# Splitting the first dense weights during the last experts, and the residual's scale and shift on VectorE

## The chip, the cores and the metric

The kernel runs on one core of a Trainium2 chip. The metric is the device time of one execution in microseconds (us), median of several runs. TensorE (PE) multiplies matrices into PSUM banks, VectorE (DVE), ScalarE (ACT) and GpSimd (POOL) do elementwise work, SyncE (SP) issues the weight transfers. Each engine works through its own queue in the order in which the program was written, and waits on semaphores of the others.

## The reference

A decoder trunk of two layers on 256 rows of width 1024, float32. Layer 0 is a retention layer, layer 1 a sparse-attention layer that reads keys and values projected from the rows after layer 0. Each layer ends with a mixture of 16 experts, two per row. Residual and norm stand behind each part:

```python
for l in range(DEPTH):                       # DEPTH = 2
    mix = retention(h, ...) if l == 0 else nsa_attention(h, ..., nsa_shared_kv(h, ...))
    h = layer_norm(ALPHA * h + mix, ln_mix_g[l], ln_mix_b[l])
    h = layer_norm(ALPHA * h + moe(h, ...), ln_ffn_g[l], ln_ffn_b[l])
```

What the change touches lies between the experts of layer 0 and the attention of layer 1: `layer_norm(..., ln_ffn_g[0], ln_ffn_b[0])`, the projections `h @ w_kv` and `h @ w_in`, and the residual `ALPHA * h` of layer 1.

## The kernel before

**Weights.** All weight matrices come as a list of chunks of 128 x 2048 float32 (1 MB): 32 dense chunks of the retention, 96 of the experts of layer 0 (six each), 18 dense chunks of the attention layer, 96 of the experts of layer 1. The class `Weights` brings them in through a ring of seven places, with more places lent for a time. `pump` (L75) issues the next transfer on SP as soon as a place is free. `self.next` counts half chunks (128 x 1024).

**Two kinds of chunk.** Expert chunks, and four dense ones, are multiplied as they are ("plain"). The other dense halves are first split into a high and a low part of the type fp32r, so that three fast matmuls replace one slow one: a copy on ACT (L114) and a subtraction on DVE (L115). The two parts go to one of four places of the pool `stage` (`self.slots`). `ahead` (L102) splits as many coming halves as there are free places, but none from `self.limit` on; `take` and `get` (L130, L139) call it each time PE's program asks for the next half and so gives back the last one's place. A split is thus written into the queues of ACT and DVE at the point where an older half is given up.

**Experts.** `experts` (L709) writes expert after expert. In round e, PE gets the matmuls of gate and up of expert e+1, with a few fillers (the transposes of the hidden rows of e, `turn`, and the scatter of expert e-1's result into the four sums `y`), then `down(e)`. The hidden rows of e+1 take one instruction on ACT (L790) and one on DVE (L791); the result of `down` is split by ACT (L217) and DVE (L218) before its scatter. While a layer's experts run, `self.limit` is 0, set in `mix_norm` (L597); behind the last expert it is lifted (L956). In layer 0 the function then calls `ahead(2, nc.gpsimd)` (L960): two halves are split with GpSimd in VectorE's role.

**Between the layers.** `next_rows` (L992) follows: 20 warming matmuls (L247), the statistics of the four sums and the reciprocal root on DVE (`block_stats`, L301 to L274), the normalised rows `res` (L1004 on ACT, L1005 on DVE), their transposes on PE (L1012), and per pair of transposes a high part on ACT (L1015) and a low part on DVE (L1017, L1021). It loads the norm's two rows `gb` through the POOL queue and returns the function that makes `res` the residual: `res * gb[0] + gb[1]` for both blocks of 128 rows.

**Attention layer, first part.** `nsa` (L1044) then runs five projections (`proj`, L322: 48 matmuls of 512 columns, four halves of weights each). Here they are called projection 1 to 5: 1 to 3 give keys and values, 4 and 5 the queries. `shift()` stands at L1231, ahead of projection 1. After projection 1 come `pairs` (ropes on DVE, L1068 to L1074, a copy on ACT, L1111), the gate weights and the router's sums; projection 2 is written behind these. Behind projection 4 the queries of block 0 get their rope on DVE; those of block 1 are copied by ACT to `qc` (L1255) and get theirs on GpSimd. `qc` takes the place (tag `q1`) that `gb` had. The residual itself is read only after the attention (L1457).

The order in each queue is the order of the program text (`manual_schedule`); nothing reorders it.

Of the kernel before, what the change touches and what calls it, by code (L numbers as in the profile page):

```python
# [23 lines left out]
NE = 16  # L24
# [129 lines left out]
class Trunk:  # L154
# [46 lines left out]
    def alloc(self, name, side="right"):  # L201

        self.extra.append(self.tc.alloc_tile_pool(name=name, bufs=1, side=side, reuse_waits="tile"))
        return self.extra[-1]

    def first_place(self, l, side):

# [501 lines left out]
    def experts(self, pool, keep, oh0, rest, hh, hl, y, l):  # L709
# [92 lines left out]
        def down(e, hT):  # L802

            b = [self.bank(), self.bank()]
            for k in range(4):
                both(hT[:, k, :], self.W.get(2)[0], b, k == 0, k == 3)
            if not out:
                out.append(self.first.tile([P, 2048], F32R, tag="raw", name=f"out{l}"))
            d = []
            for i in range(2):  # L810
                t = out[0][:, i * 512:i * 512 + 512]
                hi, lo = t[64 * i:64 * i + 64], t[64 - 64 * i:128 - 64 * i]
                self.hilo(hi, lo, b[i][64 * i:64 * i + 64, :])
                d.append(t)
            return d
# [111 lines left out]
        for e in range(NE):  # L927
            g = e // 4 + 1
            if e % 4 == 1 and g < 4:
                oh[g] = self.one_hot(keep, g, l)  # L930
                picks = gather(g)
            hT = pool.tile([P, 4, 64], F32, tag="hT", name=f"hT{l}_{e}", bufs=1)
            fill = [lambda: turn(hT)] + (scatter(e - 1, d, False) if e else [])
            if e % 4 == 0 and e:
                fill.append(lambda: turn_hot(e // 4))
            if e + 1 < NE:
                fill += more[:1] + picks[:2] + todo[:2]
                more, picks, todo = more[1:], picks[2:], todo[2:]
                b = gate_up(e + 1, fill)
                if e % 4 == 2 and g < 4:  # L940
                    weigh(g)
                hidden(e + 1, b)
            else:
                for f in fill:
                    f()
            if e == 13:
                overflow()
            d = down(e, hT)
            if e == 0:
                turn_hot(0)  # L950
            if l == 1 and e > 9 and self.gb is None and self.W.slots:
                todo += norm_rows()
        for f in todo:
            f()
        self.ready(AF.Sqrt)
        self.W.limit = 2 * len(self.W.srcs)  # L956
        for f in scatter(NE - 1, d, True):
            f()
        if l == 0:
            self.W.ahead(2, nc.gpsimd)  # L960

    def ffn(self, y, rows, keep, acc, l):

# [28 lines left out]
    def next_rows(self, pool, y, res, hTh, hTl):  # L992

        nc = self.nc
        self.gb = self.extra[0].tile([P, 2048], F32, tag="q1", name="gb1").rearrange("p (a n) -> p a n", a=2)
        nc.gpsimd.dma_start(self.gb, self.t["ln_rows"][1:2].to_broadcast([P, 2, 1024]))
        self.warm(self.bits, WARM[1])
        mv, ends = self.block_stats(pool, y, "lf0")
        rs = [f() for f in ends]
        mr = pool.tile([P, 1], F32, name="lf0_mr")  # L1000
        nc.vector.scalar_tensor_tensor(mr, mv[0][:, 0:1], -1.0, rs[0], op0=ALU.mult, op1=ALU.mult)
        for nh in range(2):
            c = slice(nh * 512, nh * 512 + 512)
            nc.scalar.activation(res[:, 0, c], y[0][nh], AF.Identity, bias=mr, scale=rs[0])  # L1004
            nc.vector.tensor_scalar(res[:, 1, c], y[1][nh], mv[1][:, 0:1], rs[1], op0=ALU.subtract, op1=ALU.mult)  # L1005
        o = W_LN + 16
        for j in range(0, 8, 2):
            b = self.bank().rearrange("p (a b) -> p a b", a=2)
            t = pool.tile([P, 2, 256], F32, tag="nt", name=f"nt{j}", bufs=2)
            for jj in range(2):  # L1010
                for tb in range(2):
                    nc.tensor.transpose(b[:, jj, tb * P:tb * P + P], res[:, tb, (j + jj) * P:(j + jj + 1) * P], self.ident)  # L1012
            gc = [[self.wsm[:, i + j + jj:i + 1 + j + jj] for i in (o, o + 8)] for jj in range(2)]
            for jj, (g, c) in enumerate(gc):
                nc.scalar.activation(hTh[:, j + jj], b[:, jj], AF.Identity, bias=c, scale=g)  # L1015
            for jj, (g, c) in enumerate(gc):
                nc.vector.tensor_scalar(t[:, jj], b[:, jj], g, c, op0=ALU.mult, op1=ALU.add)  # L1017
                if j == 0 or jj:
                    k = slice(jj if j == 0 else 0, jj + 1)
                    ks = slice(j + k.start, j + k.stop)  # L1020
                    nc.vector.tensor_sub(hTl[:, ks], t[:, k], hTh[:, ks].bitcast(F32))  # L1021
            if j == 4:
                self.W.ahead(1)
        return lambda: [self.scale_shift(nc.gpsimd, res[:, tb, :], res[:, tb, :], slice(0, 1024)) for tb in range(2)]

    def last_rows(self, pool, y):
        nc = self.nc
# [16 lines left out]
    def nsa(self, pool, norm, nq, keep):  # L1044
# [128 lines left out]
        def gate_logits():  # L1173
            b = self.bank()
            for k in range(8):
                for i, (w, x) in enumerate(((wgh, hTh), (wgh, hTl), (wgl, hTh))):
                    nc.tensor.matmul(b[0:48, 0:256], w[:, k, :], x[:, k, :], start=(k == 0 and i == 0), stop=(k == 7 and i == 2))
            ge = pr.tile([48, 256], F32, name="ge")
            nc.scalar.activation(ge, b[0:48, 0:256], AF.Exp, scale=-1.0)
            return ge  # L1180

        def set_gates(ge):
            b = self.bank()
            for tb in range(2):
                nc.tensor.transpose(b[:, tb * 48:tb * 48 + 48], ge[:, tb * P:tb * P + P], self.ident[0:48, 0:48])
            gv = flat(gates)
            nc.vector.tensor_scalar_add(gv, b[:, 0:96], 1.0)
            nc.vector.reciprocal(gv, gv)
# [3 lines left out]
        def turn_hidden(ck, cv):  # L1192
            b = self.bank()
            for a, c in enumerate((ck, cv)):
                for m in range(2):
                    nc.tensor.transpose(b[:, a * 128 + m * 64:a * 128 + m * 64 + 64], c[:, m * P:m * P + P], self.ident[0:64, 0:64])
            hk[0] = pr.tile([P, 2, 64], F32, name="hk")
            nc.vector.tensor_copy(hk[0], b[:, 0:128].rearrange("p (m r) -> p m r", m=2))
            hv[0] = pr.tile([P, 2, 4, 4, 32], F32, name="hv")
            nc.gpsimd.memset(hv[0], 0.0)  # L1200
            bv = b[:, 128:256].rearrange("p (m r) -> p m r", m=2)[:, :, 0:60].rearrange("p m (g n) -> p m g n", g=4)
            for m in range(2):
                nc.vector.tensor_copy(hv[0][:, m, :, :, 0:NCMP], bv[:, m].unsqueeze(2).to_broadcast([P, 4, 4, NCMP]))
# [24 lines left out]
        with self.phase("nkv") as pr:  # L1228
            wv = pr.tile([P, V_N], F32, name="wv")
            nc.gpsimd.dma_start(wv, self.t["w_nsa"])  # L1230
            shift()  # L1231
            KC = big.tile([P, 2048], F32, tag="q0", name="KC").rearrange("p (a g t) -> p a g t", a=2, g=4)
            b = self.proj(hTh, hTl, early=True)
            wgh, wgl = [pr.tile([P, 8, 48], F32R, name=f"wg{c}") for c in "hl"]
            kv2 = pairs(b)
            self.hilo(wgh, wgl, wv[:, V_GT:V_GT + 384].rearrange("p (k n) -> p k n", k=8))
            sums = self.router(pr, 1)
            b = self.proj(hTh, hTl)
            turn_pairs(kv2)
            t = [keys(0, tb, b[tb]) for tb in range(2)]  # L1240
            sums()
            blk = [blocks(0)]
            b = self.proj(hTh, hTl)
            for f in t:
                f()
            blk.append(blocks(1))
            t = [keys(1, tb, b[tb]) for tb in range(2)]
            ck = hidden(0, blk[0])
            cv = hidden(1, blk[1])
            ge = gate_logits()  # L1250
            QT = []
            b = self.proj(hTh, hTl, fill=[t[0], t[1], none, lambda: turn_hidden(ck, cv), lambda: set_gates(ge), none, compressed])
            t = [queries(0, 0, b[0])]
            c = big.tile([P, 2048], F32, tag="q1", name="qc")
            nc.scalar.copy(c[:, 0:512], b[1])  # L1255
            t.append(queries(0, 1, c[:, 0:512], nc.gpsimd, c[:, 512:1536]))
            t[0][0]()
            t = [t[0][1], *t[1]]
# [310 lines left out]
```

## Time and profile before

| | |
|---|---|
| median of 3 runs | 902.41 us (899.76, 902.41, 905.68) |
| profiled execution, its own time | 901.26 us |
| its span, first to last instruction | 899.4 us |
| mean granted TensorE clock | 0.977 of 2.4 GHz |
| busy in the span: PE / DVE / ACT / POOL | 849.5 / 407.7 / 339.8 / 67.4 us |

The page gives each engine's busy time, the span in 40 slices of 22.5 us, the chain of work that ended last, and the costliest groups of instructions. Two thin spots of PE stand out among the slices: the first slices of the run, and the two around 427 to 472 us. A closer look needs the timeline (instructions in order of time, with the idle time ahead of each and what ended it), short windows with the granted clock, and the instructions of one line.

### The profile page before, as it was taken

To read this page: it belongs to the slowest core of one execution; us is meant where nothing else is said; L and a number is where in the kernel's file an instruction comes from. 1 tells how busy PE (TensorE), PEld (TensorE's weight loads), DVE (VectorE), ACT (ScalarE), POOL (GpSimd) and SP (SyncE) were. 2 spreads that over 40 slices of the span, in tenths; PEclk is the share of its full clock that TensorE was granted. 3 is DMA by queue.
4 is the path that set the end of the run, shared out by engine and by line. 5 is a ranking of instruction groups with operands and counts; after the bars stand their busy time and mean duration, and the time that the engine had idled before them with its cause. 6 is when DMAs were issued, how large, how long until landed. Compare 5 with 4: busy or idle time off the path is not lost. (4 is left out here: it accounts for less than half of the span.)

```text
span 899.4 us, 12118 instructions
## 1 busy us (share of the span) xinstructions
PE 849.5 (94%) x4738; PEld 537.3 (60%) x4738; DVE 407.7 (45%) x811; ACT 339.8 (38%) x657; POOL 67.4 (7%) x76
## 2 busy tenths in 40 slices
PE   7999999998999999999779999899999999999993
PEld 5998989986545354453237777665844535445431
DVE  4667766864322222221169866885442222222215
ACT  4434344434232322322153555785433232232312
POOL 1000000001100000000036003430020000000001
PEclk8999999998999999999999899999999999999997
DMA  9956353588599999999723375303779999999901
GB/s 341 426 229 234 137 193 139 188 321 354 204 389 415 427 422 427 423 426 423 306 85 132 144 294 212 126 22 148 308 287 387 421 426 426 426 426 426 388 3 47
DMA packets 37282, 259.83 MB, mean 289 GB/s; under 512 B 4216, under 2 KB 4400, under 8 KB 6368
## 3 DMA queue, kind: packets, MB, share of 16 engines
q1 hardware_dynamic: 36432, 255.87, 70.3%
q0 software_dynamic: 640, 2.97, 1.0%
q8 instruction: 42, 0.69, 0.3%
q14 instruction: 24, 0.20, 0.1%
q10 hardware_dynamic: 144, 0.11, 0.1%
HBM read 257.88 MB, written 1.05 MB: 288 GB/s over the span
## 5 line engine op out<-in xcount | busy, mean ns | idle before, releaser
L771 PE MATMUL bank<-raw,xT 128*64 128x512 f32 x1024 | 233.9, 596 | 0.8 <-ACT xT L730 0.8
L771 PEld LDWEIGHTS bank<-raw,xT 128*64 128x64 f32 x1024 | 76.7, 137 | 125.9 <-issue 119.0
L115 DVE TENSOR_TENSOR st<-raw,st 128x1024 fp32r<-128x1024 f32 x90 | 114.9, 1304 | 51.1 <-ACT st L114 49.9
L114 ACT CAST st<-raw 128x1024 fp32r<-128x1024 f32 x92 | 94.6, 1048 | 78.0 <-PE bank L334 26.3
L771 PE MATMUL bank<-raw,hT 128*64 128x512 f32 x512 | 116.9, 594 | 7.2 <-PEq L875 3.3
L318 PE MATMUL bank<-xh,st 128*128 128x256 f32 x512 | 93.5, 284 | 3.0 <-ACT st L114 2.6
L218 DVE TENSOR_TENSOR out<-bank,out 64x512 fp32r<-64x512 f32 x64 | 44.1, 688 | 102.5 <-ACT out L217 101.5
L771 PEld LDWEIGHTS bank<-raw,hT 128*64 128x64 f32 x512 | 39.9, 137 | 74.1 <-issue 71.6
L318 PEld LDWEIGHTS bank<-xh,st 128*128 128x128 f32 x512 | 80.4, 192 | 3.6 <-ACT st L114 2.8
L217 ACT CAST out<-bank 64x512 fp32r<-64x512 f32 x64 | 37.1, 580 | 108.7 <-PE bank L771 107.9
L318 PE MATMUL bank<-xl,st 128*128 128x256 f32 x256 | 72.3, 282 | 0.0
L791 DVE SCALAR_TENSOR_TENSOR sh<-bank,wsl,sh 64x512 f32<-64x512 f32 x32 | 23.7, 741 | 105.3 <-ACT sh L790 105.1
L790 ACT ACTIVATE sh<-bank 64x512 f32<-64x512 f32 x32 | 19.0, 594 | 94.8 <-PE bank L771 94.8
L334 PE MATMUL bank<-st,hTh 128*128 128x512 f32 x128 | 45.8, 429 | 4.1 <-ACT st L114 2.2
L318 PEld LDWEIGHTS bank<-xl,st 128*128 128x128 f32 x256 | 49.4, 193 | 0.1
L351 PE MATMUL acc<-st,gh 128*128 128x512 f32 x128 | 43.2, 410 | 1.7 <-DVE st L115 1.1
L800 ACT COPY hT<-bank 128x256 f32<-128x256 f32 x32 | 12.0, 374 | 86.9 <-PE bank L799 86.8
L820 PE MATMUL y_moe<-out 128*128 128x512 f32 x128 | 38.6, 419 | 4.4 <-DVE out L218 4.4
L334 PE MATMUL bank<-st,xh 128*128 128x512 f32 x128 | 40.6, 393 | 0.0
L835 DVE SCALAR_TENSOR_TENSOR al<-bank,wsm,al 128x256 f32<-128x256 f32 x16 | 7.7, 484 | 72.1 <-ACT al L834 72.1
L728 DVE TENSOR_SCALAR xT<-bank,wsm 128x128 f32<-128x128 f32 x64 | 21.9, 405 | 34.1 <-PE bank L722 26.2
L334 PEld LDWEIGHTS bank<-st,hTh 128*128 128x128 f32 x128 | 25.7, 204 | 11.6 <-ACT st L114 2.6
(329 smaller groups left out, 1224.1 us busy)
## 6 DMA issues: line engine op xcount, KB each, us to landing
raw<-in_w_moe_dram SPq DMA_DIRECT2D x190, 1024.0 KB, 10.6
raw<-in_w_dense_dram SPq DMA_DIRECT2D x49, 1024.0 KB, 6.5
raw<-in_w_moe_dram SPq DMA_DIRECT2D x4, 512.0 KB, 15.8
xT<-in_x_T_dram SPq DMA_DIRECT2D x4, 256.0 KB, 4.6
raw<-in_w_dense_dram SPq DMA_DIRECT2D x2, 512.0 KB, 9.4
rt<-in_c_ret_dram POOLq DMA_DIRECT2D x1, 1024.0 KB, 11.1
gb<-in_ln_rows_dram POOLq DMA_DIRECT2D x1, 1024.0 KB, 6.4
out_dram<-lf_n SPq DMA_DIRECT2D x4, 256.0 KB, 2.0
```

Source lines behind the costliest of these rows:

```text
L114: self.nc.scalar.copy(hi, r)
L115: (eng or self.nc.vector).tensor_sub(lo, r, hi.bitcast(F32))
L217: self.nc.scalar.copy(hi, src)
L218: self.nc.vector.tensor_sub(lo, src, hi.bitcast(F32))
L318: self.nc.tensor.matmul(b[:, m, :], w[:, kk, c], x[:, k, :], start=(k == 0 and i == 0 and m == 0), stop=(k == 7 and i == 2 and m == 1))
L334: self.nc.tensor.matmul(b[tb], x[:, k, c], w[:, kk, :], start=(k == 0 and i == 0), stop=(k == 7 and i == 2))
L351: self.nc.tensor.matmul(y[tb][nh], x[a][:, c], w[b][:, 0, n], start=False, stop=last and i == 2)
L728: nc.vector.tensor_scalar(t, v, c, d, op0=ALU.mult, op1=ALU.add)
L771: nc.tensor.matmul(b[i][c, :], x, w[:, i, :], start=first, stop=last)
L790: nc.scalar.activation(rows[0:64], b[64:128], AF.Silu)
L791: nc.vector.scalar_tensor_tensor(rows[0:64], b[0:64], w, rows[0:64], op0=ALU.mult, op1=ALU.mult)
L820: return [lambda tb=tb, nh=nh: nc.tensor.matmul(y[tb][nh], o[:, tb, :], d[nh], start=(e == 0), stop=last) for nh in range(2) for tb in ran ...
```

## The change

Four edits:

1. New method `split_ahead(n)`: it sets the limit to n halves behind the experts of layer 0 and calls `ahead()`.
2. In layer 0, round 14 calls `split_ahead(2)` and round 15 `split_ahead(4)`, each just ahead of `down(e)`: dense halves 0 and 1, then 2 and 3, split by ACT and DVE.
3. The two splits with GpSimd behind the last expert go; the limit is lifted behind the last scatter.
4. The residual's scale and shift become two functions on VectorE, one per block of 128 rows. The first is written behind `gate_logits` and ahead of projection 4, the second as the last filler of projection 4. `shift()` ahead of projection 1, on GpSimd, goes.

```diff
+    def split_ahead(self, n):
+        self.W.limit = 2 * self.moe_end(0) + n
+        self.W.ahead()
...
             if e == 13:
                 overflow()
+            if l == 0 and e >= NE - 2:
+                self.split_ahead(2 * (e - NE + 3))
             d = down(e, hT)
...
         self.ready(AF.Sqrt)
-        self.W.limit = 2 * len(self.W.srcs)
         for f in scatter(NE - 1, d, True):
             f()
-        if l == 0:
-            self.W.ahead(2, nc.gpsimd)
+        self.W.limit = 2 * len(self.W.srcs)
...
-        return lambda: [self.scale_shift(nc.gpsimd, res[:, tb, :], res[:, tb, :], slice(0, 1024)) for tb in range(2)]
+        return [lambda tb=tb: self.scale_shift(nc.vector, res[:, tb, :], res[:, tb, :], slice(0, 1024)) for tb in range(2)]
...
             nc.gpsimd.dma_start(wv, self.t["w_nsa"])
-            shift()
             KC = big.tile([P, 2048], F32, tag="q0", name="KC").rearrange("p (a g t) -> p a g t", a=2, g=4)
...
             ge = gate_logits()
+            shift[0]()
             QT = []
-            b = self.proj(hTh, hTl, fill=[t[0], t[1], none, lambda: turn_hidden(ck, cv), lambda: set_gates(ge), none, compressed])
+            b = self.proj(hTh, hTl, fill=[t[0], t[1], none, lambda: turn_hidden(ck, cv), lambda: set_gates(ge), none, compressed, shift[1]])
```

## Rows read from the trace of the kernel before

**Rows 1.** Windows: us, busy PE, PEld, DVE, ACT, POOL; PEclk, DMA share, GB/s

```profile
468.00:470.00 2.00, 2.00 (x13) 1.77 (x11) 0.80 (x2) 1.92 (x6) 0.36 (x1) 0.61 1.00 418
474.00:476.00 2.00, 2.00 (x8) 1.57 (x7) 2.00 (x4) 0.08 (x1) 0.00 (x0) 0.69 0.00 0
...
494.00:496.00 2.00, 0.73 (x2) 0.30 (x2) 2.00 (x7) 2.00 (x3) 0.00 (x0) 0.93 0.02 4
502.00:504.00 2.00, 2.00 (x16) 1.99 (x15) 1.78 (x3) 0.96 (x2) 0.00 (x0) 0.86 0.64 270
```

**Rows 2.** Timeline behind the last expert: start, us, engine, line, operation [idle before]

```profile
459.49 1.89 DVE L301 BATCH_NORM_STATS2 lf_st<-y_moe 128x6 f32<-128x512 f32 x3
461.21 4.65 POOL L115 TENSOR_TENSOR st<-raw,st 128x1024 fp32r<-128x1024 f32 x2 [231.03 <-ACT st L114]
463.61 2.26 DVE L274 SCALAR_TENSOR_TENSOR lf_y<-lf_q,lf_y 128x1 f32<-128x1 f32 x1
466.31 0.15 DVE L1001 SCALAR_TENSOR_TENSOR lf_mr<-lf_mv,lf_y 128x1 f32<-128x1 f32 x1
467.42 2.75 PE L1012 MATMUL bank<-cst,res 128*128 128x128 f32 x16 [3.90 <-ACT res L1004]
470.77 1.19 PE L334 MATMUL bank<-st,hTh 128*128 128x512 f32 x2 [0.60 <-DVE nt L1017]
```

**Rows 3.** Chain that ended last: start, us, what (the kernel's final norm)

```profile
886.42 1.91 DVE lf_st L301 x3
...
890.74 0.15 DVE lf_mr L1033
```

**Rows 4.** Line L115 from 440 to 560 us: min/median/max ns, first and last start

```profile
L115 DVE TENSOR_TENSOR st<-raw,st x18: 1215/1227/3572, 474.3 to 546.8; 128x1024 fp32r<-128x1024 f32 x18
```

**Rows 5.** Timeline of projections 1 and 2, from 481 to 497 us

```profile
481.67 6.77 DVE L115 TENSOR_TENSOR st<-raw,st 128x1024 fp32r<-128x1024 f32 x2
...
484.08 0.39 PE L334 MATMUL bank<-st,hTh 128*128 128x512 f32 x1
484.31 0.40 PE L334 MATMUL bank<-st,hTl 128*128 128x512 f32 x1
487.44 3.26 POOL L990 TENSOR_TENSOR res<-res,gb 128x1024 f32<-128x1024 f32 x1
488.36 0.41 DVE L1068 TENSOR_TENSOR nr<-bank,rp 128x256 f32<-128x256 f32 x1
493.75 3.89 ACT L114 CAST st<-raw 128x1024 fp32r<-128x1024 f32 x4
494.85 0.50 PE L334 MATMUL bank<-st,hTh 128*128 128x512 f32 x1 [2.20 <-ACT st L114]
496.68 1.22 PE L334 MATMUL bank<-st,hTh 128*128 128x512 f32 x2 [1.10 <-DVE st L115]
```

**Rows 6.** Timeline of the last two experts, and SP's issues of dense chunks

```profile
422.49 18.62 SPq L92 DMA_DIRECT2D raw<-in_w_dense_dram  x7
448.22 0.74 DVE L791 SCALAR_TENSOR_TENSOR sh<-bank,wsl,sh 64x512 f32<-64x512 f32 x1 [7.64 <-ACT sh L790]
451.63 1.41 DVE L218 TENSOR_TENSOR out<-bank,out 64x512 fp32r<-64x512 f32 x2 [2.67 <-ACT out L217]
457.44 1.19 ACT L217 CAST out<-bank 64x512 fp32r<-64x512 f32 x2 [4.84 <-PE bank L771]
```

**Rows 7.** Window in round 14, columns as in rows 1

```profile
446.00:448.00 2.00, 2.00 (x12) 0.72 (x10) 0.00 (x0) 0.40 (x1) 0.00 (x0) 1.00 0.10 41
```

**Rows 8.** Timeline at the end of projection 4 and in projection 5

```profile
542.98 0.69 DVE L1068 TENSOR_TENSOR nr<-bank,rp 128x512 f32<-128x512 f32 x1 [1.75 <-PE bank L334]
544.48 1.74 POOL L1068 TENSOR_TENSOR qc<-qc,rp 128x512 f32<-128x512 f32 x1 [52.71 <-ACT qc L1255]
545.80 0.95 DVE L218 TENSOR_TENSOR qs<-nq,qs 128x512 fp32r<-128x512 f32 x1 [0.74 <-ACT qs L217]
547.68 1.03 PE L1097 MATMUL bank<-cst,qs 128*128 128x128 f32 x8
```

## The prediction, made before the result was known

> **What bounds the kernel now.** I read the page first: PE is busy for 849.5 of 899.4 us, so what can be won is PE's idle time and the time in which its clock is halved. Short windows over the whole span with the granted clock came next, to find the stretches below full clock; then the timeline of the stretch that the change touches, from the last experts to the first scores; then the waits.
>
> In the experts PE hardly waits, and every later stage is paced by PE too: no wait of PE on a transfer shows in layer 1. So a gain made ahead of the attention should arrive whole at the end. Two places between the layers cost PE time.
>
> The first is the norm behind the last expert. From the first statistics to the value `mr` that releases the normalised rows DVE takes 466.46 - 459.49 = 6.97 us [rows 2]. The same sequence at the end of the kernel takes 890.89 - 886.42 = 4.47 us [rows 3]. The difference lies beside GpSimd's two splits, 461.21 to 465.86: one DVE instruction on 128 single numbers lasts 2.26 us there [rows 2]. PE stands 3.90 us ahead of the transposes and then works at half clock: 0.61 in the window from 468 and 0.69 in that from 474 put the low stretch at 468.4 to 475.3 us, at the 1.2 GHz level [rows 1].
>
> The second is projection 2. While GpSimd multiplies and adds the residual, DVE's splits last 6.77 us for two [rows 5], where the median of that line is 1.23 us and its longest 3.57 [rows 4]. DVE is never idle in between and starts the ropes of `pairs` at 488.36 [rows 5], several us after projection 1 has ended. ACT's copies in `pairs` are written behind the ropes and wait for them; behind the copies in ACT's queue stands the cast of the half that projection 2 needs last. PE waits 2.20 us for the cast and 1.10 us for the subtraction [rows 5]. After that its clock is at half from 495.7 to 502.6 us (0.93 in the window from 494, 0.86 in that from 502) [rows 1].
>
> **The change part by part.**
>
> *GpSimd's two splits go.* DVE's chain falls from 6.97 to 4.47 us, as at the kernel's end: 2.50 us earlier for the transposes and for projection 1. Bounds: nothing, if something else holds the chain, to 2.50. I take 2.50, because instructions, shapes and order are the same in both chains.
>
> *Half clock in projection 1.* Before, it cost (475.3 - 470.77) / 2 = 2.25 us of projection 1 [rows 1, 2]. The idle time ahead shrinks by 2.5 us, but there is still little for PE between the warming matmuls and projection 1. So I expect the clock to fall again and take no difference. Bounds: 2.25 gained if it stays up, 1.2 lost if all of a 6.9 us stretch lies in projection 1 (3.4 instead of 2.25). By a sentence of its own, the Trainium skill (TensorE: Matmul & The Clock Gate, Part 1) has the gate not reset at a kernel's start, so that slow stretches fall differently from run to run; one trace can't show it.
>
> *GpSimd's four residual instructions go from projections 1 and 2.* DVE's splits fall back to 1.23 us each. Also, four halves are ready ahead of projection 1, so its first two splits leave DVE and ACT. The two splits from 481.67 would need 2.5 us, not 6.77, so DVE reaches the ropes when projection 1 ends, over 4 us sooner. From DVE's first rope to the cast of the late half it took 493.75 - 488.36 = 5.4 us, part of it still beside GpSimd, and the subtraction 1.2 more; PE needs that half only at the last quarter of projection 2. At full clock a matmul of 512 columns starts 0.23 us after the last (484.08, 484.31 [rows 5]), so the 36 ahead of that quarter give 8.3 us. 5.4 + 1.0 + 1.2 is 7.6, below 8.3: both waits go. That is 2.20 + 1.10 = 3.30 us [rows 5]. With them goes the low clock: 502.6 - 496.7 = 5.9 us of work at half speed, worth 2.9 us [rows 1, 5]. Sum 6.2 us. Bounds: 3.3 less if a short wait remains that still lowers the clock; nothing, if the wait stays whole.
>
> *Four splits during the last experts.* Two casts (3.89 us for four, so 1.0 each [rows 5]) and two subtractions (1.23 each [rows 4]) per round. In round 14 ACT is free once L790 has ended, about 448.2, until the result of `down`; the casts end at 450.2. DVE subtracts from 449.2 to 451.7, and its next work starts at 451.63 [rows 6]: 0.1 us late at most, and that much later for the scatter. In round 15 ACT has 4.84 us free ahead of 457.44 [rows 6]; nothing moves. The data are there: the seven dense transfers were issued from 422.49 to 441.1 [rows 6], and from 446 to 448 the transfers are down to a tenth [rows 7]. `done` now frees ring places some 14 us sooner, so SP's next dense loads go into a stretch without traffic. Cost 0.1 us; bounds 0 and 1.2 (one whole subtraction).
>
> *The residual on VectorE.* Four instructions of 128 x 1024 at 1.23 us [rows 4] are 4.9 us. The first pair lies ahead of projection 4's fillers and delays the low parts of the keys by some 2 us; they are first read by the scores in projection 5, 20 us later. What covers it is projection 4 itself: 48 matmuls whose weights are split ahead. The second pair starts when DVE is free, at 542.98 - 1.75 = 541.23, and lasts to 543.7; the ropes of the queries start at 542.98 before [rows 8]. So they are 0.7 us late, and are next read when PE turns them at 547.68, 0.93 us after the low part was ready (546.75) [rows 8]. `qc` must now wait for the pair, as it takes `gb`'s place; ACT reached it at about the same time before, so GpSimd's rope starts near 544.5 as before.
>
> Now a row against this part: beside GpSimd, DVE's instructions with two operands in SBUF were held up by 2.1 us [rows 2] and 2.3 us [rows 4]. The last addition of the rope is such an instruction. Before, it ran just ahead of GpSimd's rope; 0.7 us later it meets that instruction of 1.74 us [rows 8] and is held by some 1.3 us more. 0.7 + 1.3 - 0.93 leaves PE about 1 us short; without the hold it would be nothing. I take 0.7. Bounds: 0, and 5.8 (2.4 us of a whole pair and 3.4 us for a clock that falls on it). The Trainium skill (SBUF — State Buffer, section Who interferes with whom) has this as a rule: a DVE instruction with two SBUF inputs and a GpSimd instruction that reads SBUF exclude each other, and the one that comes second waits for all of the first. By the rule the term would be the whole 1 us, by the bare order of the rows 0.
>
> **Sum.** 2.5 + 0 + 6.2 - 0.1 - 0.7 = 7.9 us. Against the profiled execution's own time: 901.26 - 7.9 = 893.4 us. That execution lies 1.15 us below the median of the runs, 902.41; from the median it would be 894.5. I take 894.0 us, so a base of 901.9 between the two, for the rivals as well.
>
> **The rivals.**
>
> *A, the forecast:* 894.0; with the clock's terms and the rests of the waits 890.5 to 897. Chance 0.60.
>
> *B, the wait in projection 2 stays,* because the late half is queued behind the ropes on both engines anyway. Then only the norm's 2.5 us is won, less 0.8: 901.9 - 1.7 = 900.2. Against it: 7.6 us of work in 8.3 us of cover, and the 7.6 still has work beside GpSimd in it. For it: the cover is only 0.7 us longer. Chance 0.12, with all between B and A.
>
> *C, the clock doesn't fall ahead of projection 1:* another 2.25 us, 894.0 - 2.25 = 891.7. For it: PE's gap is 2.5 us shorter. Against it: the transposes alone are little work. Chance 0.17.
>
> *D, the late pair on VectorE stops PE at the turn of the queries and the clock falls there:* the 5.8 us bound instead of 0.7, so 894.0 + 5.1 = 899.1. Against it: 0.93 us of slack [rows 8], where the fall ahead of projection 1 came after an idle time of 3.90 us [rows 2]. For it: projection 5 has attention steps as fillers, each with DVE work in front. Chance 0.07.
>
> *E, slower:* ACT's cast in round 14 waits for a place in `stage`. Everything of ACT is queued behind it: the eviction of `down(14)`, the hidden rows of the last expert, and PE behind these. The gain is gone from a wait of 7.9 us on; it would come to that if a place were held until the last `down`, which ends at 457.4: 457.4 - 448.2 = 9.2 us, and half of a 6.9 us low stretch behind it, 3.4: 894.0 + 12.6 = 906.6. Against it: the places lent to expert chunks end ten chunks before the last one, so all four were read by PE before round 14. Chance 0.04.
>
> **How the numbers follow.** The range is 890.0 to 899.0: C with its clock term at the low end, D at the high end; outside lie E, most of B and the tails of C, under 0.2. About 1% (9 us, 893.4) is what a measurement of this kernel can tell from no change. A lies across that bound, a bit more than half above it (0.33 of its 0.60); C lies below it but for 0.02. Faster by over 1%: 0.27 + 0.15 = 0.42. Slower by over 1%: 0.02, half of E, where its price comes out above the one worked out. Within 1%: 0.33 + 0.02 + 0.12 + 0.07 + 0.02 = 0.56.
>
> **What would show it.** In the changed kernel's timeline: DVE's chain from the first statistics to `mr` at 4.5 us; no DVE L115 over 2 us in projections 1 and 2; no idle of PE over 1 us in projection 2 and a granted clock of 1.00 there; four splits between 448 and 456 us without a longer idle of PE ahead of the scatters; PE idle up to 1 us ahead of L1097. I am wrong if PE's idle in projection 2 remains, if the clock falls at a new place (the start of the scores), or if the gain at the start of the attention (some 8 us) is not found at the end.

## The result and the profile after

The changed kernel takes 891.68 us (median of 4 runs, 891.52 to 891.96) against 902.07 us before (4 runs, 899.76 to 905.68). The ratio is 0.9892, 95% interval 0.9875 to 0.9909: 9.7 us faster by the ratio (the two medians differ by 10.4). The prediction was 894.0 us, range 890.0 to 899.0. The profiled execution of the changed kernel has a span of 890.1 us (own time 891.96), the one before 899.4.

Five new lines at the top of the class move all later lines by five: L115 and L92 keep their numbers, L301 is now L306, L334 is L339, L1120 is L1125, and so on.

The first place, the norm behind the last expert. Timeline of the changed kernel (start, us, engine, line, operation, idle before), which answers to [rows 2]:

```profile
457.26 1.46 PE L825 MATMUL y_moe<-out 128*128 128x512 f32 x4 [1.38 <-DVE out L223]
457.96 1.89 DVE L306 BATCH_NORM_STATS2 lf_st<-y_moe 128x6 f32<-128x512 f32 x3
...
461.68 0.16 DVE L279 SCALAR_TENSOR_TENSOR lf_y<-lf_q,lf_y 128x1 f32<-128x1 f32 x1
...
462.28 0.15 DVE L1006 SCALAR_TENSOR_TENSOR lf_mr<-lf_mv,lf_y 128x1 f32<-128x1 f32 x1
...
463.38 1.97 PE L1017 MATMUL bank<-cst,res 128*128 128x128 f32 x16 [1.40 <-ACT res L1009]
...
466.74 0.70 PE L339 MATMUL bank<-st,hTh 128*128 128x512 f32 x2 [1.39 <-DVE nt L1022]
```

From the first statistics to `mr` it is now 462.43 - 457.96 = 4.47 us, to the hundredth the time at the kernel's end [rows 3]. The instruction that lasted 2.26 us beside GpSimd lasts 0.16. TensorE stands 1.40 us ahead of the transposes instead of 3.90, the 16 transposes take 1.97 us instead of 2.75, and projection 1 starts at full rate: two matmuls in 0.70 us instead of 1.19.

The second place, projections 1 and 2. Windows of the changed kernel (us, busy time of PE, PEld, DVE, ACT, POOL, then the granted clock, DMA share and GB/s), against [rows 1], the third of them for a later place:

```profile
466.00:477.00 11.00, 10.26 (x44) 8.32 (x45) 8.69 (x15) 4.98 (x8) 1.67 (x4) 1.00 0.19 52
478.00:489.00 11.00, 11.00 (x49) 8.83 (x48) 9.13 (x20) 5.58 (x7) 0.00 (x0) 1.00 0.45 168
554.00:565.00 11.00, 9.87 (x39) 6.52 (x40) 8.86 (x25) 6.24 (x25) 6.88 (x7) 0.53 0.01 1
```

The clock stays at 1.00 through both projections, and PE is busy in all of the second window. The third window belongs to the start of the attention, which comes up again under e8. Line L115 of the changed kernel from 440 to 560 us (min/median/max in ns), against [rows 4], and the timeline of the late half, against [rows 5]:

```profile
L115 DVE TENSOR_TENSOR st<-raw,st x20: 1203/1224/2286, 447.6 to 535.6; 128x1024 fp32r<-128x1024 f32 x20
```

```profile
477.63 0.42 DVE L1073 TENSOR_TENSOR nr<-bank,rp 128x256 f32<-128x256 f32 x1
...
481.07 2.00 ACT L114 CAST st<-raw 128x1024 fp32r<-128x1024 f32 x2
...
482.74 3.50 DVE L115 TENSOR_TENSOR st<-raw,st 128x1024 fp32r<-128x1024 f32 x3
...
489.20 1.91 PE L1125 MATMUL bank<-cst,kv 128*128 128x128 f32 x16
```

No split but one, at 535.6, is slow. From the first rope to the cast of the late half it is 481.07 - 477.63 = 3.4 us, not 5.4. From the start of projection 1 to the transposes behind projection 2 it is 489.20 - 466.74 = 22.46 us; before it was 30.34 (470.77 [rows 2] to 501.11). The line of before that ends it:

```profile
501.11 2.62 PE L1120 MATMUL bank<-cst,kv 128*128 128x128 f32 x16
```

The splits in the last two experts, against [rows 6]:

```profile
446.57 1.98 ACT L114 CAST st<-raw 128x1024 fp32r<-128x1024 f32 x2
446.70 0.74 DVE L796 SCALAR_TENSOR_TENSOR sh<-bank,wsl,sh 64x512 f32<-64x512 f32 x1 [7.64 <-ACT sh L795]
447.63 2.36 DVE L115 TENSOR_TENSOR st<-raw,st 128x1024 fp32r<-128x1024 f32 x2 [0.19 <-ACT st L114]
...
452.05 2.36 DVE L115 TENSOR_TENSOR st<-raw,st 128x1024 fp32r<-128x1024 f32 x2 [0.54 <-ACT st L114]
...
456.52 1.41 DVE L223 TENSOR_TENSOR out<-bank,out 64x512 fp32r<-64x512 f32 x2 [2.11 <-ACT out L222]
```

and the line of before that answers to the last of them:

```profile
458.05 1.41 DVE L218 TENSOR_TENSOR out<-bank,out 64x512 fp32r<-64x512 f32 x2 [5.01 <-ACT out L217]
```

They sit in gaps of both engines. From the hidden rows of the last expert on DVE to the split of its `down` result it is 456.52 - 446.70 = 9.82 us; before, 458.05 - 448.22 = 9.83. They cost nothing.

The late pair on VectorE and what follows it, against [rows 8]:

```profile
528.79 1.23 DVE L994 TENSOR_TENSOR res<-res,gb 128x1024 f32<-128x1024 f32 x1
530.05 1.22 DVE L995 TENSOR_TENSOR res<-res,gb 128x1024 f32<-128x1024 f32 x1
531.20 0.68 DVE L1073 TENSOR_TENSOR nr<-bank,rp 128x512 f32<-128x512 f32 x1
...
532.58 1.29 DVE L1079 TENSOR_TENSOR nq<-nr,nr 128x512 f32<-128x512 f32 x1
...
532.03 1.29 POOL L1073 TENSOR_TENSOR qc<-qc,rp 128x512 f32<-128x512 f32 x1 [57.85 <-ACT qc L1260]
...
535.76 1.09 PE L1102 MATMUL bank<-cst,qs 128*128 128x128 f32 x8 [0.38 <-DVE qs L223]
...
538.58 0.62 PE L1315 MATMUL bank<-Kc,QT 128*128 128x32 f32 x4 [0.25 <-DVE QT L1104]
```

The rope's last addition (L1079) meets GpSimd's rope and takes 1.29 us where it took 0.69; TensorE waits 0.38 and 0.25 us in places where it waited for nothing; a wait of 0.50 us that it had ahead of the second turn of the queries (551.91 us before) is gone.

Where the time went, in the two profiled executions: up to the last scatter of layer 0 the changed kernel is 1.53 us ahead (457.26 against 458.79), and e9, the same kernel again, comes to that scatter at 459.61, so that is the run and not the change; between that scatter and the last matmul of projection 5 it takes 92.00 us instead of 102.55; the rest of the span is 340.84 us against 338.06. The sum is -1.53 - 10.55 + 2.78 = -9.30 us, the difference of the spans. The lines behind these numbers are the start of the last scatter (before; after it stands above) and the last matmul of projection 5, before and after:

```profile
458.79 1.46 PE L820 MATMUL y_moe<-out 128*128 128x512 f32 x4 [1.38 <-DVE out L218]
...
561.34 0.39 PE L334 MATMUL last<-st,hTh 128*128 128x512 f32 x1
```

```profile
549.26 0.40 PE L339 MATMUL last<-st,hTh 128*128 128x512 f32 x1
```

So the gain of the change is 10.55 us, and what follows it differs by more than any wait in it. The experiments below show both parts.

### The profile page after: what moved, and what is told of

It is laid out like the page before. It is cut to its first block, busy times and chain, and to the rows that moved or that the text cites. A ratio compares the mean times of both kernels' runs of the same rounds, so it can differ in the third digit from the quotient of the medians.

```text
span 890.1 us, 12109 instructions
## 1 busy us (share of the span) xinstructions
PE 846.9 (95%) x4738; PEld 535.0 (60%) x4738; DVE 405.6 (46%) x817; ACT 339.7 (38%) x657; POOL 50.0 (6%) x70
## 5 line engine op out<-in xcount | busy, mean ns | idle before, releaser
L115 DVE TENSOR_TENSOR st<-raw,st 128x1024 fp32r<-128x1024 f32 x92 | 111.4, 1234 | 55.4 <-ACT st L114 55.3
L339 PE MATMUL bank<-st,hTh 128*128 128x512 f32 x128 | 42.2, 401 | 1.7 <-DVE nt L1022 1.4
L825 PE MATMUL y_moe<-out 128*128 128x512 f32 x128 | 38.6, 419 | 4.4 <-DVE out L223 4.4
L339 PE MATMUL bank<-st,xh 128*128 128x512 f32 x128 | 40.5, 393 | 0.0
L735 ACT ACTIVATE xT<-bank,wsm 128x128 f32<-128x128 f32 x64 | 24.1, 456 | 19.3 <-PE bank L727 19.3
```

Source lines behind the costliest of these rows:

```text
L115: (eng or self.nc.vector).tensor_sub(lo, r, hi.bitcast(F32))
L339: self.nc.tensor.matmul(b[tb], x[:, k, c], w[:, kk, :], start=(k == 0 and i == 0), stop=(k == 7 and i == 2))
L735: nc.scalar.activation(t, v, AF.Identity, bias=d, scale=c)
L825: return [lambda tb=tb, nh=nh: nc.tensor.matmul(y[tb][nh], o[:, tb, :], d[nh], start=(e == 0), stop=last) for nh in range(2) for tb in ran ...
```

## The experiments

The comparisons below use one number for the part that the change touches: the time from the start of the last scatter (L820 before, L825 after) to the start of the last matmul of projection 5, read from each trace's timeline. It is free of what a run does before and behind. The ratio stands beside it. Each stage is read from one trace of its kernel. The diffs are cut (`...`) and stand against the changed kernel where nothing else is said; comments in them are mine.

| kernel | stage, us | against before | ratio of times (95%) |
|---|---|---|---|
| before | 102.55 | | |
| changed | 92.00 | -10.55 | 0.9892 (0.9875 to 0.9909) |
| e1 splits only | 97.94 | -4.61 | 0.9946 (0.9927 to 0.9965) |
| e2 residual only | 96.51 | -6.04 | 0.9921 (0.9895 to 0.9946) |
| e3 splits behind the expert, on VectorE | 96.44 | -6.11 | 0.9926 (0.9905 to 0.9947) |
| e4 residual early, on VectorE | 91.61 | -10.94 | 0.9869 (0.9847 to 0.9891) |
| e5 as e2, more warming | 94.51 | -8.04 | 0.9897 (0.9876 to 0.9918) |
| e6 residual late, on GpSimd | 95.98 | -6.57 | 0.9926 (0.9902 to 0.9949) |
| e7 both pairs behind projection 4 | 94.37 | -8.18 | 0.9899 (0.9880 to 0.9918) |
| e8 as e4, idle matmuls in the attention | 91.66 | -10.89 | 0.9868 (0.9849 to 0.9888) |
| e9 changed, again | 92.01 | -10.54 | 0.9886 (0.9866 to 0.9906) |
| e10 two halves ahead | 92.01 | -10.54 | 0.9884 (0.9866 to 0.9902) |
| e11 as e4, again | 91.61 | -10.94 | 0.9874 (0.9852 to 0.9897) |
| e12 as e8, again | 91.61 | -10.94 | 0.9882 (0.9865 to 0.9900) |

My theory is that GpSimd's instructions hold up VectorE's wherever the two meet, and that this made both losses. The rivals: depth (what counts is that four halves are ready), place (what counts is that work leaves the stretch between norm and projection 2), and, for TensorE's clock, that a late start alone costs the time.

### e1: the splits alone

```diff
-            shift[0]()          # ahead of projection 4, and shift[1] as its last filler
+            shift()             # ahead of projection 1, as before
```

The line that returns the four instructions has `nc.gpsimd` again.

> The change's first half alone: four halves split during the last two experts, none on GpSimd behind them; the residual's scale and shift stay on GpSimd ahead of projection 1. Theory (GpSimd's instructions hold up VectorE's): the norm's chain from the first statistics to mr falls from 6.97 to 4.47 us, but VectorE's splits beside the residual still take 3 us and more, so a wait of TensorE of 1 to 3 us and a low clock remain in projection 2: 3 to 6 us faster than before. Rival (depth: what counts is that projection 1 starts with four halves ready): no wait in projection 2, 8 us or more faster.

The chain of the norm is 4.47 us long (458.06 to 462.53), the clock holds in projection 1, and yet TensorE waits in projection 2 as it did before. Timeline of e1, PE:

```profile
488.95 0.59 PE L339 MATMUL bank<-st,hTh 128*128 128x512 f32 x1 [2.29 <-ACT st L114]
490.79 1.22 PE L339 MATMUL bank<-st,hTh 128*128 128x512 f32 x2 [0.82 <-DVE st L115]
```

The two waits sum to 3.11 us (3.30 before) and the clock is at half from 489.2 to 496.0 us. Four ready halves don't help against GpSimd's residual: depth falls as the cause of the second loss.

### e2: the residual alone

```diff
-            if l == 0 and e >= NE - 2:
-                self.split_ahead(2 * (e - NE + 3))
...
+        if l == 0:
+            self.W.ahead(2, nc.gpsimd)
```

> The change's second half alone: the residual late on VectorE; the two splits with GpSimd stay behind the last expert. Theory: no wait over 1 us in projection 2 and no low clock there, the norm's chain stays at 7.0 us: 5 to 7 us faster than before. Rival (depth): the late half in projection 2 is still late, under 3 us faster.

No wait in projection 2 and no low clock there; the norm is as long as before. Timeline of e2:

```profile
459.36 1.89 DVE L301 BATCH_NORM_STATS2 lf_st<-y_moe 128x6 f32<-128x512 f32 x3
...
466.17 0.15 DVE L1001 SCALAR_TENSOR_TENSOR lf_mr<-lf_mv,lf_y 128x1 f32<-128x1 f32 x1
467.27 2.77 PE L1012 MATMUL bank<-cst,res 128*128 128x128 f32 x16 [3.89 <-ACT res L1004]
```

6.96 us from the first statistics to the end of `mr`, TensorE idle for 3.89 us, and a clock at half from 468.3 to 475.1 us, all as before. The two halves of the change add up: 4.61 + 6.04 = 10.65 us of stage, 10.55 together.

### e3: the two splits behind the last expert, on VectorE

```diff
-            if l == 0 and e >= NE - 2:
-                self.split_ahead(2 * (e - NE + 3))
...
+        self.W.limit = 2 * len(self.W.srcs)
         for f in scatter(NE - 1, d, True):
             f()
-        self.W.limit = 2 * len(self.W.srcs)
+        if l == 0:
+            self.W.ahead(2)
```

> The changed kernel, but its first two splits stand behind the last expert again, with VectorE for the subtraction instead of GpSimd; no splits during the experts. Theory: without GpSimd no instruction of the norm is held up, but ScalarE's cast and two subtractions of 1.2 us now stand ahead of the statistics on VectorE: mr some 3 us later than in the changed kernel, 3 to 5 us slower than it, 5 to 8 us faster than before. Rival (only GpSimd's hold counts, the subtractions hide behind the scatter): within 1 us of the changed kernel.

```profile
458.02 1.45 PE L825 MATMUL y_moe<-out 128*128 128x512 f32 x4 [1.38 <-DVE out L223]
...
462.73 1.89 DVE L306 BATCH_NORM_STATS2 lf_st<-y_moe 128x6 f32<-128x512 f32 x3
...
467.05 0.15 DVE L1006 SCALAR_TENSOR_TENSOR lf_mr<-lf_mv,lf_y 128x1 f32<-128x1 f32 x1
```

Once it has started, the chain takes 4.47 us here too (462.73 to 467.20): without GpSimd nothing in it is held up. But it starts 4.71 us behind the scatter instead of 0.70, because the two splits stand ahead of it on VectorE. The stage is 4.44 us longer than in the changed kernel, of which 4.01 are that later start. So the splits had to leave this place, not only GpSimd; the rival falls. The delay was larger than the 3 us I expected. TensorE stands 5.41 us ahead of the transposes, and the clock is at half from 467.7 to 471.1 us: it is back before projection 1 begins at 471.96.

### e4: the residual on VectorE, at its old place

```diff
             nc.gpsimd.dma_start(wv, self.t["w_nsa"])
+            shift[0]()
+            shift[1]()
...
-            shift[0]()          # and no shift[1] in the fillers of projection 4
```

> The changed kernel, but the residual's four instructions stand on VectorE at their old place ahead of projection 1. Theory (the engine counts, not the place): 4.9 us of VectorE in projection 1, where it has gaps; the half that projection 2 needs last comes at most 1 us late; no wait at the turn of the queries: within 1 us of the changed kernel. Rival (the place counts: anything between the norm and projection 2 delays the late half): a wait of 2 us or more and a low clock in projection 2, 4 us or more slower than the changed kernel.

Timeline of e4: the four instructions, the splits behind them, and the turn of the queries.

```profile
472.07 1.22 DVE L994 TENSOR_TENSOR res<-res,gb 128x1024 f32<-128x1024 f32 x1
...
475.72 1.22 DVE L995 TENSOR_TENSOR res<-res,gb 128x1024 f32<-128x1024 f32 x1
476.87 3.49 DVE L115 TENSOR_TENSOR st<-raw,st 128x1024 fp32r<-128x1024 f32 x3
...
535.39 1.03 PE L1102 MATMUL bank<-cst,qs 128*128 128x128 f32 x8
```

VectorE does the whole residual in 4.9 us during projection 1. Its ropes start 2.4 us later than in the changed kernel, and still the late half comes in time. TensorE waits neither in projection 2 nor at the first turn of the queries (ahead of the second it waits 0.51 us, as before the change), and the stage is 0.39 us shorter than in the changed kernel. The engine counts and the late place doesn't: the place rival falls, and the change's move to projection 4 costs 0.4 us without giving anything. The lead of 2 us in the ratio is not all from here (e11).

### e5: the clock in projection 1

Kernel e2, in which `mr` comes late, with more work for TensorE in the gap.

```diff
-WARM = 10, 20, 20, 12
+WARM = 10, 42, 20, 12
```

> The kernel with the residual late on VectorE alone (splits with GpSimd behind the last expert, so mr late), with 42 instead of 20 warming matmuls ahead of the transposes: 22 x 0.17 = 3.8 us of work for TensorE, which fills the 3.9 us for which it stands idle there. Theory (the idle time before projection 1 is what lowers the clock): the granted clock stays at 1.00 through projection 1, which starts at the same time and ends 2.3 us sooner; 2 to 3 us faster than with 20. Rival (the late start itself is all that costs): the same time as with 20, within 0.5 us.

```profile
460.06 7.00 PE L247 MATMUL bank<-bits 128*128 128x384 bf16 x42
...
467.39 1.97 PE L1012 MATMUL bank<-cst,res 128*128 128x128 f32 x16 [0.33 <-ACT res L1004]
```

The clock stays at 1.00, the transposes take 1.97 us instead of 2.77, and the stage is 2.00 us shorter than in e2, although projection 1 starts no sooner behind the scatter (11.98 us; 11.97 in e2). So the low clock of projection 1 has a price of its own, some 2 us, and it comes from the idle time ahead of it. The rival, that the late start is all that costs, falls.

The other traces fit. The clock fell ahead of projection 1 where TensorE stood 3.89 to 5.41 us ahead of the transposes (before, e2, e3): for 6.8 us before and in e2, for 3.4 us in e3. It fell in none of the traces with 1.40 us there or less: the changed kernel, e1, e4, and e5 to e12.

### e6: the residual at the late places, on GpSimd

```diff
-        return [lambda tb=tb: self.scale_shift(nc.vector, ...
+        return [lambda tb=tb: self.scale_shift(nc.gpsimd, ...
```

> The changed kernel with the residual's four instructions at their new, late places, but on GpSimd. Theory (GpSimd's hold on VectorE and its length count where VectorE is near its limit): no wait in projection 2, so still over 6 us faster than before; but GpSimd's pair behind projection 4 takes some 4.8 us, the copy to qc waits for it, and the queries of block 1 come 1 to 3 us late: 1 to 3 us slower than the changed kernel. Rival (the engine doesn't matter once the place is late): within 0.5 us of the changed kernel.

The outcome was neither. Timeline of e6:

```profile
477.12 2.41 POOL L994 TENSOR_TENSOR res<-res,gb 128x1024 f32<-128x1024 f32 x1
...
486.31 2.46 POOL L995 TENSOR_TENSOR res<-res,gb 128x1024 f32<-128x1024 f32 x1
...
477.58 6.39 DVE L115 TENSOR_TENSOR st<-raw,st 128x1024 fp32r<-128x1024 f32 x2 [0.61 <-ACT st L114]
...
486.55 2.51 DVE L1115 COPY kv<-kr 128x512 f32<-128x512 f32 x1
...
491.87 0.50 PE L339 MATMUL bank<-st,hTh 128*128 128x512 f32 x1 [1.42 <-ACT st L114]
493.71 1.22 PE L339 MATMUL bank<-st,hTh 128*128 128x512 f32 x2 [1.10 <-DVE st L115]
```

The program has the four instructions behind `gate_logits` and behind projection 4, but GpSimd's queue is empty and nothing that they need is late, so they run from 477 to 489 us all the same, beside projections 1 and 2. VectorE's splits take 6.39 us for two, a copy of VectorE takes 2.51 us (the same line takes 0.43 us at 490.28, when GpSimd is done), and both waits of TensorE are back, 1.42 and 1.10 us, with 3.4 us at half clock from 493.2. The stage is 3.98 us longer than in the changed kernel. My expectation had taken the place in the program for a time. What it shows for the question: with GpSimd in the same stretch the loss returns, whatever the place in the program.

### e7: both pairs behind projection 4

```diff
-            shift[0]()
...
-..., compressed, shift[1]])
+..., compressed, lambda: (shift[0](), shift[1]())])
```

> The changed kernel with both pairs on VectorE behind projection 4: 2.4 us more ahead of the ropes. Theory (the slack at the turn of the queries is used up by the one pair, which left TensorE a wait of 0.4 us): TensorE waits 2.8 us there; 2.4 us slower than the changed kernel, up to 5.8 with a low clock. Rival (slack left): within 0.5 us of it.

```profile
538.70 1.09 PE L1102 MATMUL bank<-cst,qs 128*128 128x128 f32 x8 [2.77 <-DVE qs L223]
```

2.77 us against the 2.8 expected, the stage 2.37 us longer than in the changed kernel, and the clock did not fall at that wait. No slack is left behind projection 4: the second pair, 2.4 us on VectorE, costs TensorE 2.39 us more of waiting.

### e10: two halves ahead instead of four

```diff
-            if l == 0 and e >= NE - 2:
-                self.split_ahead(2 * (e - NE + 3))
+            if l == 0 and e == NE - 1:
+                self.split_ahead(2)
```

> The changed kernel with only two halves split ahead, in the last round, as many as before the change but without GpSimd. Theory (it is GpSimd's hold that counts, not that four halves are ready): the norm's chain stays at 4.5 us, the two other splits find room beside the norm and projection 1; within 1 us of the changed kernel. Rival (depth): a wait of 1 us or more in projection 1 or 2, over 2 us slower than it.

92.01 us of stage against 92.01 for the changed kernel beside it (e9). The two splits more are worth nothing: depth falls for good.

e9 is the changed kernel itself once more, on one chip with e10, e11 and e12:

> The changed kernel itself, beside the next three on one chip, to read small differences. From the last expert's last scatter to the last matmul of projection 5 it should take 92.0 us as in its first trace (102.6 before), with no low clock in projections 1 and 2; 9 to 11 us faster than before.

It came so: 92.01 us of stage, no low clock in projections 1 and 2, and 10.0 us faster than before by the medians.

### e8, e11 and e12: the clock at the attention's start

In each trace up to e7, TensorE waits 2.9 us for VectorE in the attention's first turn (555.13 us in the changed kernel), beside GpSimd's ropes for the second half of the queries. Around that wait the clock falls, in the changed kernel from 554.4 to 564.7 us (0.53 in the third window above). e8 is e4 with idle matmuls in the wait:

```diff
...
+                    if first and r == 3:                       # first turn of unit 0
+                        for _ in range(17):
+                            nc.tensor.matmul(d[:, 0:384], self.bits[:, 0:P], self.bits, start=True, stop=True)
```

> The kernel with the residual early on VectorE, with 17 idle matmuls (2.9 us) ahead of the last transpose of the attention's first turn, where TensorE waits 2.9 us for VectorE in every trace so far. Theory (that idle time lowers the clock for 3.4 to 10.2 us, differently from run to run, and makes most of the spread): the clock stays at 1.00 around the attention's start; 1.7 to 5 us faster than without the fill, and its runs lie within 1 us except for other places. Rival (VectorE and ScalarE pace that stretch, not TensorE): within 1 us of the kernel without the fill.

Windows and timeline of e8:

```profile
552.00:563.00 11.00, 9.53 (x62) 6.11 (x63) 10.69 (x27) 6.95 (x29) 9.53 (x10) 1.00 0.21 85
```

```profile
552.74 2.93 PE L1372 MATMUL fill<-bits 128*128 128x384 bf16 x17
555.85 0.33 PE L1373 MATMUL tb<-cst,pt 128*128 128x128 f32 x1 [0.18 <-DVE pt L1356]
...
561.25 0.71 PE L1386 MATMUL ob<-pTc,VC 128*128 128x128 f32 x4 [1.29 <-ACT pTc L1366]
```

The clock stays up, and TensorE comes to a new wait of 1.29 us some 5 us later; VectorE is busy for 10.69 of the 11 us. So that stretch is VectorE's, and the ratio hardly differs from e4's: the rival holds, and the 1.7 to 5 us that I expected did not come.

VectorE's instructions are stretched there beside GpSimd, as they were at the first two places. In the changed kernel:

```profile
552.51 1.26 POOL L1079 TENSOR_TENSOR nq<-nr,nr 128x512 f32<-128x512 f32 x1
552.58 1.27 DVE L1320 TENSOR_TENSOR pc<-sc,mn 128x64 f32<-128x64 f32 x1
...
554.11 1.65 DVE L1355 TENSOR_SCALAR pt<-pt,cf 128x128 f32<-128x128 f32 x2
...
555.13 0.48 PE L1366 MATMUL tb<-cst,pt 128*128 128x128 f32 x1 [2.92 <-DVE pt L1355]
```

Some us earlier, with GpSimd idle, L1320 took 0.23 us and two of L1355 0.47. By these rows GpSimd's ropes hold up the very instructions for which TensorE waits 2.92 us. No run takes the ropes away from GpSimd, so what that would give is not shown.

What the clock is worth there shows when the traces are sorted by the time at half clock at the attention's start, read from windows of 1 us, against the rest of the span behind the last matmul of projection 5:

| low clock there, us | rest of the span, us |
|---|---|
| 0 (e8, e12) | 338.14, 338.05 |
| 3.4 (before, e1, e3, e7, e10) | 338.06, 338.1, 338.14, 338.11, 338.02 |
| 6.8 (e4, e5, e9, e11) | 339.63, 339.63, 339.58, 339.61 |
| 10.2 (changed, e2, e6) | 340.84, 340.93, 340.48 |

3.4 us at half clock cost nothing against the two filled kernels, 6.8 cost 1.5 us, 10.2 cost 2.4 to 2.9. The code there is the same in all but e8 and e12, and the changed kernel itself has 10.2 in its first trace and 6.8 in e9. So which row a run falls in is the run's and not the change's: a spread of up to 2.9 us.

e11 is e4 once more and e12 is e8 once more.

> The changed kernel with the residual on VectorE at its old, early place. Theory: no wait at the turn of the queries, 0.4 us less up to the end of projection 5; the rest of the 1 us by which it led in its first runs is the clock at the attention's start. 0 to 1.5 us faster than the changed kernel. Rival: no difference.

> The same with 17 idle matmuls ahead of the last transpose of the attention's first turn. Theory now: the clock stays up there, which is worth nothing against a low stretch of 3.4 us and 1.5 to 2.7 us against one of 6.8 or 10.2, so about 1 us in the median and fewer slow runs. Rival: no difference.

The traces say 0.40 us for the early place (92.01 against 91.61), and the fill stays clear of the two lower rows of the table. The times on one chip, 891.61 (e9), 890.59 (e10), 890.68 (e11) and 890.80 us (e12), have ratios whose intervals overlap: by time the four can't be told apart. e4 and its kin beat both kernels by the traces; against the changed kernel that is 0.4 us, less than the times can show.

## Why the prediction was right, and where it was not

**The norm: right.** Predicted 2.50 us, measured 6.97 - 4.47 = 2.50; projection 1 starts 9.48 us behind the last scatter instead of 11.98. e3 and e2 show both halves of the reason: without GpSimd the chain takes 4.47 us wherever it starts, with its splits 6.96.

**The clock in projection 1: the term that was mis-sized.** I took 0 between bounds of a loss of 1.2 and a gain of 2.25 us, as I thought the clock would fall all the same. It didn't, and the upper bound of the gain came true: in the changed kernel projections 1 and 2 have 1.00 throughout, and the time from the start of projection 1 to the transposes behind projection 2 is 7.88 us shorter, 3.30 of it idle time and 4.58 clock, of which the row of before gives 2.25 to projection 1. That was rival C, which I gave 0.17, at 891.7 us; the measured median is 891.68. The match to 0.02 us is luck: C's sum is 10.15 us, the stage gained 10.55, and the profiled execution lost 2.78 behind it. e5 shows that the term is real and apart from the start: 2.00 us with the start unchanged. The step that failed is the reading of the gap, which put at 0 a term that measured 2.25. I counted the transposes as little work and the gap as still long, where rows of the trace could have made me doubt it: TensorE also stands 1.38 us ahead of the last scatter, and the clock is at full behind that. The Trainium skill's sentence, that slow stretches fall differently from run to run (TensorE: Matmul & The Clock Gate, Part 1), fits the attention's start, where the same code has 3.4, 6.8 or 10.2 us of it; in projection 1 it fits the length of the stretch only (6.8, 6.8 and 3.4 us in the three traces with a long gap). Whether the clock fell there did not differ from run to run: in all three with a long gap, in none of the eleven with a short one.

**The waits in projection 2: right.** Predicted 6.2 us. Idle 3.30, clock in projection 2 some 2.3 (4.58 - 2.25), and 2.62 - 1.91 = 0.71 at the transposes behind it: 6.3. The cover held: the late half was split by about 483.9 us, and TensorE came to it at about 486.4, and from the first rope to the cast it took 3.4 us, not 5.4. e1 and e6 show that it is GpSimd's residual in that stretch, e10 that it isn't the number of ready halves, e4 that it isn't the place in the program.

**The splits in the experts: right.** 0.1 us predicted, nothing measured; their places were free, so rival E's wait did not come.

**The late pair: right in kind, too large.** 0.7 us predicted with the mechanism named, a rope's addition held by GpSimd's instruction. It is held (1.29 instead of 0.69 us), TensorE waits 0.38 and 0.25 us, and against e4 the place costs 0.39 us of stage. I had the addition held by some 1.3 us of an instruction of 1.74; it lasted 0.60 us longer than before, as that instruction was already 0.55 us into its 1.29. The Trainium skill has the shared port as an exclusive lock (SBUF — State Buffer, Who interferes with whom), and the trace agrees: 0.74 us of the instruction were left. Rival D did not come: even the wait of 2.77 us in e7 left the clock up.

**Rival B,** the wait that stays, is what e1 and e6 look like; it needs GpSimd in the stretch.

**The way to the end: a premise too strong.** I took every later stage as paced by TensorE. At the attention's start VectorE paces it: before the change too TensorE waits 2.93 us for it there (567.22 us). The gain arrives whole all the same where the low stretch there is as long as before: the rest of the span is 338.02 us in e10 and 338.06 before. One of my signs of being wrong was a clock that falls at a new place, the start of the scores. It fell in that stage before the change too, for 3.4 us; the 10.2 us of the changed kernel's first trace are not the change's doing, as e9 has 6.8 and e10 3.4.

**The sum.** The terms as measured are 2.50 + 2.25 + 6.3 - 0.4 = 10.65 us, and the stage is 10.55 us shorter; a wait in projection 3 that grew from 0.19 to 0.35 us makes up most of the rest. 7.9 was short of it by the clock of projection 1 and 0.3 of the late pair. The profiled execution gave 2.78 us of it back behind the change, by 10.2 instead of 3.4 us of low clock at the attention's start, and had 1.53 us more ahead of it. So the near agreement of the spans' difference (9.30) with the times' (9.7) is partly chance; the stage is the number to trust.

## What to carry to other kernels

Elementwise work given to an idle GpSimd is not free where VectorE works on operands in SBUF at the same time: here it stretched splits of 1.22 us to over 3 us, and a 0.16 us step of a serial chain to 2.26 us. Before moving work in a program, ask which queue it then waits in: on an engine with an empty queue a later line is no later time (e6), while on a busy one each microsecond counts (e7). When a gap ahead of dense matmuls gets shorter, price the clock behind it as a term of its own, and when small gains are compared, measure the stage between two events and not the whole run.

## What the runs showed of the hardware

I had not expected that a low clock could be free: at the attention's start 3.4 us at half clock cost nothing against full clock, as VectorE paced the stretch (busy 10.69 of 11 us in e8, and 10.79 from 555 to 566 us in e10, which has the 3.4 us), and only longer ones cost 1.5 and 2.4 to 2.9 us.

Nor that an idle time of 1.40 us with 16 transposes behind it and another 1.39 us would leave the clock at full in the eleven traces that have that or less (0.33 us in e5), while 3.89 us (before, e2) and 5.41 us (e3) with the same transposes lowered it. A wait of 2.77 us among 512-column matmuls (e7) left it up too; one of 2.92 us at the attention's start, with short matmuls around it, lowered it in each trace without the fill. The length of one wait does not decide it: in e6 two waits of 1.42 and 1.10 us in projection 2, close together, came with 3.4 us at half clock. No run separates the length of a wait from what TensorE does around it.
